# Streaming the second half of an adaLN weight beside a projection, letting DMA issues go first on GpSimd, and putting a layer norm's affine part last

## The chip, the cores and the metric

The kernel runs on all eight cores of one Trainium2 chip, with no traffic between the cores. Times are device microseconds of the slowest core. Before the change the time was 824.52 us, the median of three runs (823.72 to 826.96). An execution has now and then a slower state, in which the cores of one die or of both run at a lower granted clock; such runs are called slow here, are listed, and are not used for comparisons.

Engines: TensorE (PE in the profile, PEld its weight loads), VectorE (DVE), ScalarE (ACT), GpSimd (POOL) and SyncE (SP).

## The reference, cut to what matters

One layer of a flow-matching backbone. Per core: one latent sequence of 1024 tokens and two context sequences of 256, model width 1024, feed-forward width 2816.

```python
# mod = SiLU(cond) @ w_ada + b_ada             w_ada is 1024 x 6144: twelve slabs of 512 columns
sh1, sc1, g1, sh2, sc2, g2 = jnp.split(mod, 6, axis=-1)
h = x * (1 + sc1) + sh1                        # slabs 0 to 3
proj = h @ p['w_in']                           # q, k, v, g of four retention heads | z, x, B, C, dt of the SSD group
...                                            # retention heads; Mamba-2 SSD heads, a chunked scan over 64-token chunks
mix = jnp.concatenate([o_ret, o_ssd], axis=-1) @ p['w_out']
x = layer_norm(ALPHA * x + g1 * mix, p['ln1_g'], p['ln1_b'])       # g1: slabs 4, 5
h2 = x * (1 + sc2) + sh2                                           # slabs 6 to 9
ffn = (jax.nn.silu(h2 @ p['w_gate']) * (h2 @ p['w_up'])) @ p['w_down']
x = layer_norm(ALPHA * x + g2 * ffn, p['ln2_g'], p['ln2_b'])       # g2: slabs 10, 11
```

Outputs are the new context and latent activations and the final retention and SSD states of the context (oret and ossd in the profile).

## The kernel before

The program is written as a list of operations in one order, and a small list scheduler inside the kernel file orders them. It keeps one clock per engine, and each time it lets the engine take the ready operation with the lowest key (level, position in the list). From that it fixes, at build time, the order of each engine and all semaphore waits. Buffers are then placed in one SBUF arena by their planned lifetimes, and each reuse of bytes adds a dependency. A planned order that the chip doesn't follow in time is not mended at run time: an engine waits for the next instruction in its order (start_restored_wo_early below has a case of 7.18 us).

```python
def add(self, alts, reads, writes, table=None, after=()):
    o = Op(len(self.ops), alts, (self.level, len(self.ops)), self.tag)    # the key
...
def dma(self, eng, out, in_, after=(), is_out=False):
    v = out if isinstance(out, View) else in_
    o = self.add({eng: (0.9 if eng == POOL else 0.45, lambda e: e.dma_start(...))}, [in_], [out], after=after)
...
P.tag, P.level = "start", 0                     # constants, x, the first weights, their arithmetic
...
LV_EV, LV_MIX, LV_DENSE, LV_BG = 0, 1, 2, 3     # evictions, scans, dense products, background
```

The large weights come in as slabs, most of 128 x 4096 elements, cast from fp32 in memory to bf16 by DMAs that GpSimd issues, at level 3 after the start and at level 0 in it. GpSimd also does arithmetic: the SSD state updates at level 1, LN1's multiply and add at level 3. The parts that the change touches:

```python
ada_load(4, [last_mm[0]]);  ada_load(5, [last_mm[1]])      # after the last product of a w_in slab
gate_row(0, 0);  gate_row(0, 1)                            # gate1: 8 matmuls of 2 x 512 each
...
rrg, rstS = Ring("rg", 3, 512), Ring("stS", 1, 512)        # retention gate; staging of the final states
...
for h in range(4):                                          # context heads
    last_h.append(head(GA, h, head_load(GA, h, [...]), LV_DENSE))
    if h < 2:
        ada_load(6 + h, [last_h[h - 1] if h else last_mm[1]])
        ada_load(8 + h, [last_h[h - 1] if h else last_mm[2]])
        mod2(h)                                             # shift2 and scale2: 2 x 32 matmuls of 128 x 2
    else:
        ada_load(8 + h, [last_h[h - 1]])
        gate_row(1, h - 2)
wo_load(0);  wo_load(1)                                     # w_out, released by last_h[2]
...                                                         # SSD of the latents, latent heads, out projection
P.level = LV_BG
ln1 = P.buf("ln1", 2048)
P.dma(SP, ln1, brow(R_LN1G, 2048), after=[oB])
for g in (GA, GB):
    for t in TT[g]:
        tt(x1[t], x1[t], ln1[:, 0:1024], ALU.mult, POOL)    # LN1's affine part: 24 instructions of 128 x 1024
        tt(x1[t], x1[t], ln1[:, 1024:2048], ALU.add, POOL)
ffn("all", LV_DENSE, [[hb[4]], [hb[4]], [oB]])              # 11 gate/up slabs (w_gu)
```

## Time and profile before

| what | value | where from |
|---|---|---|
| time, median of 3 | 824.52 us | runs |
| cores | 811.3 to 822.5 us | the profile's list of cores |
| mean granted TensorE clock | 0.945 to 0.960 | the same |
| PE idle on the slowest core | 110.2 us | 822.5 - 712.3 |
| PE idle in the start, until the projections run | 39.1 us | median of the cores, PE timelines and windows |
| PE idle from there to the third w_gu issue / from there to PE's end | 43.2 / 17.0 us | the same |

The head of the page has PE's busy time and the span cut into forty slices of 20.6 us. A digit is the busy tenths of the slice; PEclk is the granted clock, DMA the mean share of the sixteen DMA engines.

```profile
PE 712.3 (87%) x4432; PEld 373.0 (45%) x4432; DVE 398.1 (48%) x810; ACT 295.2 (36%) x470; POOL 304.1 (37%) x353
...
PE   0199999997982679899999799499999999999994
...
PEclk9999899999895789899999899799999999999998
DMA  8997132003979695202813300632266450301111
```

PE has two holes after the start, at the thirteenth slice (247 to 267 us) and at the twenty-sixth (514 to 535 us), and in both the clock drops as well. The DMA engines are at three tenths or less in slices five to ten (82 to 206 us), and at six to nine tenths in the five after those. The chain of waits says the same by engine:

```profile
PE 77%; DMA 11%; DVE 5%; issue 4%; ACT 1%; POOL 1%; SPq 0%; DVEq 0%; POOLq 0%; ACTq 0%
```

### The profile page before, as it was taken

The numbers are of one execution on the slowest core, as the hardware profiler recorded it, in microseconds if no ns is written. First come the engines' busy times: TensorE is split into PE (matmuls) and PEld (weight loads), VectorE is DVE, ScalarE is ACT, GpSimd is POOL, SyncE is SP. The second block draws the span as 40 slices with busy tenths as digits, with TensorE's granted clock in tenths as the row PEclk, the third lists the DMA queues.
The fourth block names the chain that finished last, engine by engine and source line by source line (L and its number), as shares of the span: only waits on it lengthen the run. The fifth ranks groups of instructions, "written<-read, shape, count | busy, mean of one in ns | idle before, by whom it ended". The sixth has DMA issues, their size and how long they took to land.

```text
span 822.5 us, 13372 instructions; the slowest of 8 cores (811.3 to 822.5 us)
## 1 busy us (share of the span) xinstructions
PE 712.3 (87%) x4432; PEld 373.0 (45%) x4432; DVE 398.1 (48%) x810; ACT 295.2 (36%) x470; POOL 304.1 (37%) x353
## 2 busy tenths in 40 slices
PE   0199999997982679899999799499999999999994
PEld 0168555554560334565544444144444444444441
DVE  4326547489771228888857822012222222266644
ACT  3545665676451343364554611012111111022211
POOL 9300124398451102455412699100000000058665
PEclk9999899999895789899999899799999999999998
DMA  8997132003979695202813300632266450301111
GB/s 163 204 258 129 48 53 65 1 16 53 161 130 168 156 161 149 41 13 53 179 37 125 96 1 1 96 57 52 52 122 124 101 122 1 71 26 77 78 52 77
DMA packets 19907, 73.35 MB, mean 89 GB/s; under 512 B 6000, under 2 KB 8432, under 8 KB 14208
## 3 DMA queue, kind: packets, MB, share of 16 engines
q0 software_dynamic: 6192, 44.65, 31.9%
q1 hardware_dynamic: 13648, 27.85, 10.5%
q8 instruction: 37, 0.61, 0.3%
q14 instruction: 30, 0.25, 0.1%
HBM read 108.74 MB, written 8.40 MB: 142 GB/s over the span
## 4 chain that ended last, share of the span: by engine, by line
PE 77%; DMA 11%; DVE 5%; issue 4%; ACT 1%; POOL 1%; SPq 0%; DVEq 0%; POOLq 0%; ACTq 0%
PE psum L607 74%; DMA arena<-x 4%; DMA oret<-arena 4%; PE psum L610 3%; DVE arena L655 2%; ACT arena L632 1%; DMA arena<-w_ada 1%; DMA arena<-w_gu 1%; DVE arena L669 1%; POOL arena L655 1%; DVE arena L689 1%; DVE arena L661 0%; SPq L182 0%; DVE arena L680 0%; DVEq L501 0%
## 5 line engine op out<-in xcount | busy, mean ns | idle before, releaser
L607 PE MATMUL psum<-arena 128*128 128x512 bf16 (+7 forms) x4228 | 685.6, 321 | 85.4 <-DMA arena<-w_ada 20.4
L607 PEld LDWEIGHTS psum<-arena 128*128 128x128 bf16 (+1 forms) x4228 | 346.7, 101 | 420.2 <-issue 129.5
L655 POOL TENSOR_TENSOR arena<-arena 128x512 f32<-128x512 f32 (+5 forms) x203 | 248.6, 1244 | 189.7 <-DVE arena L661 71.7
L632 ACT ACTIVATE arena<-psum 128x512 bf16<-128x512 f32 (+1 forms) x198 | 111.3, 572 | 298.1 <-PE psum L607 286.8
L655 DVE TENSOR_TENSOR arena<-psum,arena 128x512 f32<-128x512 f32 (+4 forms) x208 | 128.2, 636 | 106.7 <-PE psum L607 87.0
L655 DVE TENSOR_TENSOR arena<-arena,psum 128x512 bf16<-128x512 bf16 (+2 forms) x124 | 82.9, 676 | 197.2 <-PE psum L607 181.6
L632 ACT ACTIVATE arena<-arena 128x512 f32<-128x512 f32 (+7 forms) x121 | 86.5, 732 | 166.0 <-DVE arena L669 131.9
L669 DVE SCALAR_TENSOR_TENSOR arena<-arena 128x1 f32<-128x1 f32 (+2 forms) x108 | 62.8, 588 | 18.8 <-POOL arena L655 12.8
L632 ACT ACT_TABLE_LOAD x40 | 51.3, 1283 | 30.8 <-PE psum L607 24.5
L632 ACT ACTIVATE arena<-psum,arena 128x512 bf16<-128x512 f32 (+3 forms) x75 | 47.2, 649 | 27.3 <-PE psum L610 19.0
L182 POOL DMA_DIRECT2D arena<-w_gu x11 | 6.1, 556 | 122.4 <-PE psum L607 116.8
L610 PE MATMUL psum<-arena 128*128 128x128 f32 (+1 forms) x204 | 30.8, 305 | 13.8 <-DMA arena<-x 8.2
L680 DVE CAST arena<-psum 128x512 bf16<-128x512 f32 (+2 forms) x38 | 21.8, 590 | 31.0 <-PE psum L607 23.8
L655 DVE TENSOR_TENSOR arena<-arena 128x1 f32<-128x1 f32 (+9 forms) x74 | 31.7, 432 | 8.9 <-ACT arena L632 2.8
L610 PEld LDWEIGHTS psum<-arena 128*128 128x128 f32 (+1 forms) x204 | 26.8, 157 | 17.8 <-issue 15.9
L661 POOL TENSOR_SCALAR arena<-arena 128x128 bf16<-128x128 f32 (+2 forms) x42 | 23.2, 563 | 17.1 <-ACT arena L632 10.7
L182 POOL DMA_DIRECT2D arena<-w_ada x12 | 7.2, 605 | 54.7 <-PE psum L607 53.7
L182 POOL DMA_DIRECT2D arena<-w_down x4 | 2.1, 529 | 61.3 <-PE psum L607 61.2
L182 POOL DMA_DIRECT2D arena<-w_in x11 | 6.3, 574 | 49.6 <-PE psum L610 24.7
L661 DVE TENSOR_SCALAR arena<-arena 128x128 bf16<-128x128 f32 (+5 forms) x73 | 19.4, 304 | 9.5 <-ACT arena L632 6.8
L689 DVE TENSOR_SCALAR arena<-psum,arena 128x512 bf16<-128x512 f32 x21 | 16.6, 806 | 14.3 <-PE psum L610 14.2
L1174 DVE COPY_PREDICATED psum<-arena,psum 128x512 f32<-128x512 uint16 x24 | 16.6, 691 | 8.9 <-PE psum L607 8.8
(18 smaller groups left out, 60.7 us busy)
## 6 DMA issues: line engine op xcount, KB each, us to landing
arena<-w_ada POOLq DMA_DIRECT2D x12, 1024.0 KB, 17.8
arena<-x SPq DMA_DIRECT2D x24, 512.0 KB, 18.1
arena<-w_in POOLq DMA_DIRECT2D x11, 1024.0 KB, 22.4
arena<-w_gu POOLq DMA_DIRECT2D x11, 1024.0 KB, 12.5
arena<-w_down POOLq DMA_DIRECT2D x4, 1408.0 KB, 15.8
y<-arena SPq DMA_DIRECT2D x11, 512.0 KB, 2.6
arena<-gsc SPq DMA_DIRECT2D x4, 512.0 KB, 9.4
arena<-w_out POOLq DMA_DIRECT2D x2, 1024.0 KB, 19.5
```

Of the source, the lines that this page charges most:

```text
L182: o = self.add({eng: (0.9 if eng == POOL else 0.45, lambda e: e.dma_start(out=R(out), in_=R(in_)))}, [in_], [out], after=after)
L607: return P.add({PE: (c, lambda e: e.matmul(R(out), lhsT=R(lhsT), rhs=R(rhs), start=start, stop=stop))}, [lhsT, rhs], [out])
L610: return P.add({PE: (0.12, lambda e: e.transpose(out=R(out), in_=R(in_), identity=R(ident_f)))}, [in_, ident_f], [out])
L632: fn = lambda e: e.activation(out=R(out), in_=R(in_), func=func, **{k: R(v) for k, v in kw.items()})
L655: fn = lambda e: e.tensor_tensor(out=R(out), in0=R(in0), in1=R(in1), op=op)
L661: fn = lambda e: e.tensor_scalar(out=R(out), in0=R(in0), scalar1=R(s1), scalar2=None, op0=op0)
L669: fn = lambda e: e.scalar_tensor_tensor(out=R(out), in0=R(in0), scalar=R(scalar), in1=R(in1), op0=op0, op1=op1, **{k: R(v) for k, v in kw. ...
L680: alts[g] = (vcost(g, out, [in_], "copy"), lambda e: e.tensor_copy(out=R(out), in_=R(in_)))
L689: lambda e: e.tensor_scalar(out=R(out), in0=R(in_), scalar1=R(scale), scalar2=R(bias), op0=ALU.mult, op1=ALU.add))
L1174: P.add({DVE: (0.7, lambda e, eb=eb, ef=ef, mk_=mk_: e.copy_predicated(R(eb), R(mk_), R(ef)))}, [mk_, ef, eb], [eb])
```

## The change

The intent is to read the second half of w_ada (slabs 4 to 11) while the z projection and the SSD stage keep PE busy and the DMA engines idle, rather than in a heap beside the context heads; to keep loads from standing behind arithmetic on GpSimd; and to move LN1's affine part out of the way of the gate/up loads. Two rings and the release of w_out are adjusted.

```diff
     def dma(self, eng, out, in_, after=(), is_out=False):
         v = out if isinstance(out, View) else in_
+        lv, self.level = self.level, 0.5
         o = self.add({eng: ...}, [in_], [out], after=after)
+        self.level = lv
...
-    ada_load(4, [last_mm[0]])
-    ada_load(5, [last_mm[1]])
-    gate_row(0, 0)
-    gate_row(0, 1)
+    used = [last_mm[0], last_mm[0]]
+
+    def ada_next(s):
+        ada_load(s, [used[-2]])
+
+    for half in range(2):
+        ada_next(4 + half)
+        used.append(gate_row(0, half))          # gate_row and mod2 now return their last products
+    for half in range(2):
+        ada_next(6 + half)
+        ada_next(8 + half)
+        used += mod2(half)
+    for half in range(2):
+        ada_next(10 + half)
+        used.append(gate_row(1, half))
...
-    rsq, rrg, rqf = Ring("sq", 2, 512, BF16), Ring("rg", 3, 512), Ring("qf", 3, 512, BF16)
+    rsq, rrg, rqf = Ring("sq", 2, 512, BF16), Ring("rg", 2, 512), Ring("qf", 3, 512, BF16)
...
-    rstS, rS1, rS0 = Ring("stS", 1, 512), ...
+    rstS, rS1, rS0 = Ring("stS", 4, 512), ...
...
-        wo[half] = slab_load("wo%d" % half, w_out_d[half], 4096, after=[last_h[2]])...
+        wo[half] = slab_load("wo%d" % half, w_out_d[half], 4096, after=[last_h[3]])...
...                                             # in the loop of the context heads:
-        if h < 2:
-            ada_load(6 + h, ...); ada_load(8 + h, ...); mod2(h)
-        else:
-            ada_load(8 + h, ...); gate_row(1, h - 2)
...
     P.dma(SP, ln1, brow(R_LN1G, 2048), after=[oB])
+    P.level = 4
     for g in (GA, GB):
```

More of the change, by code (lines that the diff above doesn't have):

```diff
@@ L973, in gate_row @@
         for kt in range(8):
-            mm(ps[0:2, :], scv3[:, kt, :], wv[:, kt, :], kt == 0, kt == 7)
+            o = mm(ps[0:2, :], scv3[:, kt, :], wv[:, kt, :], kt == 0, kt == 7)
         P.level = LV_EV
@@ L979, in gate_row @@
         gdma[(which, half)] = P.dma(SP, gsc_d[which * 2:which * 2 + 2, hs], gs[0:2, 0:512])
+        return o
     def mod2(half):
         P.level = 1.2
+        n0 = len(P.ops)
         sh2[half] = mod_cols("sh2_%d" % half, 6 + half, "dense")
@@ L994, in mod2 @@
         scale2[half], bias2[half] = s_, b_
+        return [P.ops[n0 + 31], P.ops[n0 + 64]]
     def to_tm(g):
@@ L1220, in build @@
     rPT = Ring("PT", 2, 2048, BF16)
-    rsq, rrg, rqf = Ring("sq", 2, 512, BF16), Ring("rg", 3, 512), Ring("qf", 3, 512, BF16)
+    rsq, rrg, rqf = Ring("sq", 2, 512, BF16), Ring("rg", 2, 512), Ring("qf", 3, 512, BF16)
     epsb = P.buf("epsb", 1)
     memset(epsb, EPS)
-    rstS, rS1, rS0 = Ring("stS", 1, 512), Ring("S1", 2, 256, BF16), Ring("S0", 2, 256)
+    rstS, rS1, rS0 = Ring("stS", 4, 512), Ring("S1", 2, 256, BF16), Ring("S0", 2, 256)
     def ret_unit(h, ck, o0, nt, W, qT, kT, v3, gT, cross):
@@ L1335, in wo_load @@
         P.level = LV_BG
-        wo[half] = slab_load("wo%d" % half, w_out_d[half], 4096, after=[last_h[2]])[0].rearrange("p (k n) -> p k n", k=8)
+        wo[half] = slab_load("wo%d" % half, w_out_d[half], 4096, after=[last_h[3]])[0].rearrange("p (k n) -> p k n", k=8)
     ln2 = P.buf("ln2", 2048)
@@ L1462, in build @@
         last_h.append(head(GA, h, head_load(GA, h, [(last_mm[1], last_mm[2], last_h and last_h[0], last_h[1:] and last_h[1])[h]]), LV_DENSE))
-        if h < 2:
-            ada_load(6 + h, [last_h[h - 1] if h else last_mm[1]])
-            ada_load(8 + h, [last_h[h - 1] if h else last_mm[2]])
-            mod2(h)
-        else:
-            ada_load(8 + h, [last_h[h - 1]])
-            gate_row(1, h - 2)
     wo_load(0)
```

## The prediction

> **What bounds the kernel now.** The time is 824.52 us, the profiled span 822.5 us on core 3. I read first the page: TensorE (PE) is busy 87% and the chain that ended last runs on PE for 77%. So the question is where PE is not busy, or busy at a low clock. Waits by releaser, PE as the waiter, before any ordering in time:
>
> ```profile
> PE psum L607 <- DMA arena<-w_ada: 20.4, 4, 7.3
> ...
> PE psum L607 <- DMA arena<-w_gu: 10.8, 1, 10.8
> ...
> PE psum L607 <- POOL arena L655: 9.1, 4, 4.1
> PE psum L607 <- DMA oret<-arena: 9.0, 1, 9.0
> ...
> PE psum L607 <- DMA arena<-w_in: 4.8, 1, 4.8
> ```
>
> The columns are total us, times, longest. A total mixes places, so I went to the PE timeline (start, busy; in brackets the idle time before):
>
> ```profile
> 206.95 8.87 PE L607 MATMUL psum<-arena 128*2 128x512 bf16 x58 [2.86 <-DMA arena<-w_ada]
> ...
> 251.81 0.99 PE L607 MATMUL psum<-arena 128*128 128x2 bf16 x32 [3.48 <-DMA arena<-w_ada]
> 257.60 2.29 PE L607 MATMUL psum<-arena 128*128 128x512 bf16 x5 [4.79 <-DMA arena<-w_in]
> 268.84 9.74 PE L607 MATMUL psum<-arena 128*128 128x128 bf16 x67 [8.95 <-DMA oret<-arena]
> ...
> 529.68 30.55 PE L607 MATMUL psum<-arena 128*128 128x512 bf16 x132 [10.81 <-DMA arena<-w_gu]
> ```
>
> Two of the four w_ada waits lie at 23 and 31 us, in the start, which this change leaves alone (14.1 us); only 2.86 + 3.48 us are of the second half. The windows show the stages (span, then busy time of PE, weight loads, DVE, ACT, POOL; granted clock, DMA share, GB/s):
>
> ```profile
> 110.00:176.00 66.00, 65.61 (x497) 37.23 (x496) 39.18 (x64) 41.00 (x71) 32.83 (x37) 1.00 0.20 42
> 176.00:240.00 64.00, 55.83 (x553) 33.28 (x551) 56.43 (x92) 35.53 (x63) 45.63 (x57) 0.92 0.58 95
> 240.00:285.00 45.00, 21.14 (x203) 12.48 (x202) 10.53 (x26) 14.73 (x26) 7.75 (x13) 0.73 0.85 160
> 285.00:345.00 60.00, 50.88 (x300) 26.39 (x301) 35.23 (x78) 19.23 (x31) 13.13 (x15) 0.86 0.58 114
> ...
> 470.00:530.00 60.00, 49.19 (x229) 22.19 (x228) 12.07 (x18) 9.70 (x16) 47.90 (x24) 0.94 0.14 23
> 530.00:812.00 282.00, 281.46 (x1296) 127.09 (x1294) 91.45 (x184) 50.07 (x81) 68.69 (x63) 0.99 0.33 72
> ```
>
> From 110 to 176 us PE is full while the DMA engines are 80% idle; from 240 to 285 us it is the reverse. The slabs are read late and all at once. POOL's timeline says why:
>
> ```profile
> 195.03 1.56 POOL L655 TENSOR_TENSOR arena<-arena 128x512 f32<-128x512 f32 x2
> 196.55 0.66 POOL L182 DMA_DIRECT2D arena<-w_ada  x1
> 197.20 0.55 POOL L182 DMA_DIRECT2D arena<-w_in  x1
> ...
> 460.00 56.22 POOL L655 TENSOR_TENSOR arena<-arena 128x1 f32<-128x1 f32 x25 [1.78 <-DVE arena L661]
> 519.47 1.68 POOL L182 DMA_DIRECT2D arena<-w_gu  x3 [3.26 <-PE psum L607]
> ```
>
> The issues at 196.55 have no idle time before them: they stood behind arithmetic in POOL's fixed order, and so did three w_gu loads, behind 56 us of LN1's multiply and add. PE ran out of gate/up weights at 518.9 us, before the first of those was even issued.
>
> **What the Trainium skill says.** "TensorE: Matmul & The Clock Gate", section Part 1 (The HAM clock gate), has PE at half clock after an idle window of about 3.4 us and full again after one of busy time. This trace agrees: the granted clock is 0.51 and 0.50 in the slices 250 to 260 and 260 to 270 us, and after the w_gu wait 132 matmuls took 30.55 us, 0.231 each, against 281.79 us / 1296 = 0.217 in the chain after it. So a removed wait gives back more than itself. The same section would have a sustained all-core load run at 13/16 clock; here 530 to 812 us is granted 0.99, so I fear no penalty for a denser PE. "GPSIMD Engine Reference", section 2.1, describes one instruction stream dispatched in order, which is the line above: a load cannot pass an add. "DMA: Bandwidth & Descriptors", section Issuing engines are not separate DMA queues, says that all issuers share 16 engines and interleave: the oret write issued on SP at 237.79 us, behind three slabs issued in the 5 us before it, held PE until 268.84.
>
> **The change part by part.** No arithmetic is added or removed; eight w_ada slabs, 24 LN1 instructions and all loads change places.
>
> 1. *FFN start.* The w_gu loads no longer stand behind LN1. The fourth slab can go when the first is used up. A slab is 96 matmuls x 0.217 = 20.8 us of PE, so that is about two slabs, some 40 us, before it is needed; landing took 10.07 us alone. The wait of 10.81 goes, and so does the slow clock after it, 132 x (0.231 - 0.217) = 1.8. LN1's 56 us move into the following 210 us before the down projection (norms from about 725 us), where POOL does almost nothing. Gain 12 to 13 us, near certain; the other cores show the same wait, 8.9 to 14.0 us.
>
> 2. *Slabs 5 to 11 of w_ada and the head weights.* At the start, four slabs follow one another at about 8 us each (PE waits end at 15.19, 23.44, 31.29). Slab 4 goes at 111.8 us already; the rest now follow in pairs, each released by the product two before it. Four pairs at 16 us plus a PE slot, some 72 us, end near 185 us; with two head slabs, near 200. The 110 to 176 window has 53 us of idle DMA, 176 to 200 another 20: it just fits. In the old order the last w_ada went at 279 us. Their products (32 small matmuls in 0.99 us; four gate rows of 8 x 0.217 = 1.7 us) only change places. Head 0's weights go before 196.55 us, and later heads have the queue to themselves.
>
> 3. *The stage 176 to 345 us.* Idle PE time is 8.2 + 23.9 + 9.1 = 41.2 us. Low clock, by 10 us slices (busy x (1 - clock)) from 200 to 310 us: 2.3 + 1.3 + 1.6 + 0.6 + 1.9 + 1.0 + 1.9 = about 10.5. Together about 52 us that are not work. Directly removed: 2.86 + 3.48 + 4.79 (loads) and 8.95 (oret: its staging buffer goes from one to four, so the matmul that needs it does not wait for the write), 20 us, with perhaps 7 of the clock. Of the remaining 21 us idle, waits like 3.94 and 4.08 us on POOL at a retention unit's end are there because no other matmul stood ready in PE's order; with the next head's weights in, some get filled. I take 5 to 10. Sum 32 to 37 us; less 4 for costs below: about 31.
>
> 4. *Small costs.* The rg ring goes from three to two (units come some 10 us apart and its chain is about 4 us: nothing, perhaps 1 us). w_out waits for the last context head rather than the third: two slabs landed in 19.5 us (median), against some 20 us of SSD and latent-head work: 0 to 4 us. About ten issues of 0.6 us move into POOL's dense stretch (170 to 190 us: 10.00 and 9.97 busy of 10): up to 4 us of state updates delayed.
>
> Sum: 12.5 + 31 = 43.5; 824.5 - 43.5 = 781.
>
> **Rivals.**
> *SSD slows down.* PE order and POOL order are both fixed. If a slab lands later than planned, PE stalls in a stretch that was full, and a load on POOL that waits for that product holds up the state updates behind it. Also, SSD's state loads and writes (3.0 and 3.1 us now) would sit behind slabs as oret did. For it: POOL is full at 170 to 190 us, oret took 31 us. Against: SSD has head matmuls beside it. It would eat 15 to 25 of part 3: 796 to 806.
> *DVE becomes the bound.* It is busy 56.4 of 64 us at 176 to 240. But over 176 to 345 it has 102 us of 169; shortened by 33 it is 75% of the time. Locally it caps what SSD can hide: then only the 20 direct us come, 793.
> *The transfers were hidden anyway*, and PE waits next on what stood behind. For the start's w_ada waits this is so by position; for 240 to 285 us, with DVE and ACT both under a third busy, it is not. If it were, only part 1 remains: 812.
> *All gaps close*: 52 + 12.5 gives 760.
>
> **Range and chances.** Part 1 is worth 12.5 +- 2; part 3 runs from 12 (SSD slowed) to 46. So 764 to 801, centre 780. The 2% line is 808; to miss it part 3 must give less than 4 us: 5%. Slower by over 2% would need a new stall of 30 us: 1%.
>
> **What would show it.** Right: no PE wait on w_gu, and POOL's LN1 instructions spread after 470 us; DMA share at 110 to 176 us up from 0.20 to about 0.9 and no w_ada issue after about 200 us; no PE wait on oret; PE idle between 176 and the end of that stage under 20 us, clock there above 0.95; the FFN matmuls starting about 30 us earlier, at near 440. Wrong: new PE waits on w_ada or sssd at 120 to 200 us, POOL idle on PE before its issues with DVE waiting on POOL, or a PE wait on w_out after the context heads.

## The result, and the profile after

The changed kernel took 773.07 us, the median of four runs (769.09 to 774.86). The kernel before took 825.74 beside it (median of four, 823.72 to 827.31). The ratio is 0.9357, with a 95% interval of 0.9309 to 0.9405: faster, and within the predicted range. Ratios here are the mean time of one kernel's fast runs over that of the other's in the same rounds, so not quite the ratio of the medians that are quoted. One ratio does not follow from this, that of ln_waits_for_transposes; it is spoken of there. All outputs are right.

The head of the page of the changed kernel, on its slowest core (core 2), and the line of its chain of waits:

```profile
PE 688.2 (89%) x4358; PEld 367.7 (48%) x4432; DVE 394.3 (51%) x806; ACT 290.7 (38%) x466; POOL 310.3 (40%) x361
...
PE   0059999899999988899997999999999999999993
...
PEclk9979889999999999999999999999999999999998
DMA  9985805698337575226326032333775504012112
...
PE 81%; DMA 7%; DVE 5%; issue 4%; POOL 1%; ACT 1%; SPq 0%; DVEq 0%; POOLq 0%; ACTq 0%
```

Both holes are gone and the clock stays at 9 from the seventh slice to the last but one. The DMA engines work at slices seven to ten (116 to 193 us), where they had been nearly idle. But the third slice, 39 to 58 us, now has a 5: a hole at the start that wasn't there. PE's busy time fell from 712.3 to 688.2 with the same work (4432 weight loads in both). Part of that is the better clock, and part that 74 matmul records are missing here, so this difference isn't used below.

PE's waits by releaser, on the same core (total us, times, longest):

```profile
PE psum L609 <- DMA arena<-w_ada: 22.6, 2, 12.8
PE psum L612 <- DMA arena<-x: 15.5, 1, 15.5
PE psum L609 <- DVE arena L657: 8.7, 5, 5.5
...
PE psum L609 <- DMA ossd<-arena: 2.2, 1, 2.2
...
PE psum L609 <- DMA arena<-w_in: 1.4, 1, 1.4
```

There is no wait on w_gu, none on oret, and the two on w_ada are both in the start (12.79 and 9.81 us in the PE timeline). After the start only 2.2 us on an SSD write and 1.4 us on a head slab are waits on a transfer on this core. No core waits on oret or w_gu; one waits 0.3 us on w_ada, and cores 1, 5 and 6 wait 1.8 to 2.2 us on w_out, which the prediction had named as a sign of being wrong. The windows of the middle, with the columns of the prediction's windows:

```profile
110.00:176.00 66.00, 62.74 (x499) 34.92 (x508) 34.97 (x74) 37.44 (x62) 22.63 (x26) 0.94 0.68 116
176.00:240.00 64.00, 60.41 (x539) 36.04 (x544) 48.59 (x77) 39.24 (x69) 45.48 (x55) 1.00 0.51 92
240.00:285.00 45.00, 40.21 (x380) 25.80 (x385) 38.87 (x68) 29.39 (x50) 22.88 (x28) 1.00 0.65 138
285.00:345.00 60.00, 55.62 (x390) 31.66 (x395) 54.18 (x106) 27.70 (x45) 32.54 (x37) 1.00 0.42 88
```

The DMA share of the first row went from 0.20 to 0.68. The same moments hold other work now, since everything comes earlier, so the rows are read as a whole: PE's idle time in the other three is 3.6 + 4.8 + 4.4 = 12.8 us where it had been 41.2, and the granted clock of each is 1.00 where it had been 0.92, 0.73 and 0.86. The first row lost a little: its idle time went from 0.4 to 3.3 us and its clock from 1.00 to 0.94. GpSimd's timeline shows where the loads went:

```profile
121.67 1.26 POOL L183 DMA_DIRECT2D arena<-w_ada  x2 [22.94 <-PE psum L609]
...
183.01 0.59 POOL L183 DMA_DIRECT2D arena<-w_ada  x1
...
425.83 16.20 POOL L657 TENSOR_TENSOR arena<-arena 128x1024 f32<-128x1024 f32 x7 [1.31 <-DMA arena<-rows]
441.98 0.62 POOL L183 DMA_DIRECT2D arena<-w_gu  x1
442.62 13.86 POOL L657 TENSOR_TENSOR arena<-arena 128x1024 f32<-128x1024 f32 x6
458.24 0.59 POOL L183 DMA_DIRECT2D arena<-w_gu  x1 [1.76 <-PE psum L609]
```

The last w_ada load is issued at 183.0 us, where it had been at 279. The w_gu loads go between LN1's instructions rather than after all of them.

The cores differ by several us, so I compare the stages by the median of the eight cores. The next table is worked out from each core's timelines: the moment at which the projections start, the fifth w_ada load is issued, and so on, in us.

| kernel | projections start | 5th w_ada | last w_ada | w_out | first latent head's slab | 1st w_gu | 3rd w_gu | PE's end |
|---|---|---|---|---|---|---|---|---|
| before | 48.7 | 110.1 | 275.9 | 276.5 | 278.0 | 386.8 | 447.4 | 807.8 |
| changed | 57.1 | 118.9 | 178.2 | 267.2 | 249.6 | 347.0 | 408.6 | 755.1 |
| changed, again | 56.3 | 117.2 | 175.8 | 265.5 | 247.3 | 344.5 | 406.7 | 755.6 |

The start lost 8.8 us up to the fifth w_ada load. From there to the third w_gu load it was 337.3 us and is 289.7: 47.6 less. From there to PE's end it was 360.4 and is 346.5: 13.9 less. The sum is 8.8 - 47.6 - 13.9 = -52.7, which is the end's 807.8 to 755.1.

So the time came out some 7 us below the prediction, and two errors of opposite sign lie behind that: the middle gained more than foretold, and the start, which I had called untouched, lost. That they nearly cancelled is luck. PE's timeline there, of the kernel before (core 3) and of the changed one (core 2):

```profile
31.29 0.99 PE L607 MATMUL psum<-arena 128*128 128x2 bf16 x32 [6.86 <-DMA arena<-w_ada]
40.46 3.65 PE L610 MATMUL psum<-arena 128*128 128x128 f32 x16 [8.18 <-DMA arena<-x]
```

```profile
23.59 0.99 PE L609 MATMUL psum<-arena 128*128 128x2 bf16 x32 [9.81 <-DMA arena<-w_ada]
40.09 3.32 PE L612 MATMUL psum<-arena 128*128 128x128 f32 x16 [15.51 <-DMA arena<-x]
43.24 0.94 PE L609 MATMUL psum<-arena 128*128 128x2 bf16 x32
49.64 0.99 PE L609 MATMUL psum<-arena 128*128 128x2 bf16 x32 [5.46 <-DVE arena L657]
51.05 3.65 PE L612 MATMUL psum<-arena 128*128 128x128 f32 x16 [0.42 <-DVE arena L657]
```

The groups of 32 are the products of the first four w_ada slabs, the groups of 16 the transposes of x. Before, the third of the four products ran at 31.29 us, ahead of the transposes; now it stands behind them in PE's order, and the fourth then waits 5.46 us on DVE. Nothing in the start was edited. But the start's operations have level 0, and the line `self.level = 0.5` put its DMAs behind level 0 rather than ahead, and the scheduler drew another order of everything from there.

### The profile page after: what moved, and what is told of

It is laid out like the page before. It is cut to its first block, busy times and chain, and to the rows that moved or that the text cites. A ratio compares the mean times of both kernels' runs of the same rounds, so it can differ in the third digit from the quotient of the medians.

```text
span 770.4 us, 13287 instructions; the slowest of 8 cores (764.3 to 770.4 us)
## 1 busy us (share of the span) xinstructions
PE 688.2 (89%) x4358; PEld 367.7 (48%) x4432; DVE 394.3 (51%) x806; ACT 290.7 (38%) x466; POOL 310.3 (40%) x361
## 4 chain that ended last, share of the span: by engine, by line
PE 81%; DMA 7%; DVE 5%; issue 4%; POOL 1%; ACT 1%; SPq 0%; DVEq 0%; POOLq 0%; ACTq 0%
PE psum L609 78%; DMA arena<-x 5%; PE psum L612 2%; DVE arena L657 2%; DMA arena<-w_in 2%; POOL arena L657 1%; ACT arena L634 1%; DVE arena L671 1%; DMA ossd<-arena 1%; DVE arena L691 1%; SPq L183 0%; DVE psum L1190 0%; DVE arena L682 0%; POOL arena L663 0%; DVEq L503 0%
## 5 line engine op out<-in xcount | busy, mean ns | idle before, releaser
L609 PE MATMUL psum<-arena 128*128 128x512 bf16 (+9 forms) x4154 | 662.6, 316 | 51.0 <-DMA arena<-w_ada 22.6
L609 PEld LDWEIGHTS psum<-arena 128*128 128x128 bf16 (+3 forms) x4228 | 342.4, 100 | 367.7 <-issue 72.4
L657 POOL TENSOR_TENSOR arena<-arena 128x512 f32<-128x512 f32 (+5 forms) x207 | 252.1, 1236 | 181.0 <-ACT arena L634 59.8
L634 ACT ACTIVATE arena<-psum 128x512 bf16<-128x512 f32 (+2 forms) x197 | 110.0, 569 | 257.4 <-PE psum L609 236.7
L657 DVE TENSOR_TENSOR arena<-psum,arena 128x512 f32<-128x512 f32 (+5 forms) x208 | 127.4, 635 | 63.2 <-PE psum L609 52.0
L634 ACT ACTIVATE arena<-psum,arena 128x512 bf16<-128x512 f32 (+3 forms) x72 | 45.0, 645 | 34.2 <-PE psum L612 23.4
L612 PE MATMUL psum<-arena 128*128 128x128 f32 (+1 forms) x204 | 28.7, 295 | 18.9 <-DMA arena<-x 15.5
L682 DVE CAST arena<-psum 128x512 bf16<-128x512 f32 (+2 forms) x39 | 23.6, 620 | 30.0 <-PE psum L609 23.4
L657 DVE TENSOR_TENSOR arena<-arena 128x1 f32<-128x1 f32 (+9 forms) x70 | 27.8, 403 | 8.5 <-ACT arena L634 4.1
L691 DVE TENSOR_SCALAR arena<-psum,arena 128x512 bf16<-128x512 f32 x24 | 18.8, 808 | 22.9 <-PE psum L612 22.6
L663 DVE TENSOR_SCALAR arena<-arena 128x1 f32<-128x1 f32 (+7 forms) x69 | 16.5, 281 | 8.3 <-ACT arena L634 5.4
```

Source lines behind the costliest of these rows:

```text
L609: return P.add({PE: (c, lambda e: e.matmul(R(out), lhsT=R(lhsT), rhs=R(rhs), start=start, stop=stop))}, [lhsT, rhs], [out])
L612: return P.add({PE: (0.12, lambda e: e.transpose(out=R(out), in_=R(in_), identity=R(ident_f)))}, [in_, ident_f], [out])
L634: fn = lambda e: e.activation(out=R(out), in_=R(in_), func=func, **{k: R(v) for k, v in kw.items()})
L657: fn = lambda e: e.tensor_tensor(out=R(out), in0=R(in0), in1=R(in1), op=op)
L663: fn = lambda e: e.tensor_scalar(out=R(out), in0=R(in0), scalar1=R(s1), scalar2=None, op0=op0)
L682: alts[g] = (vcost(g, out, [in_], "copy"), lambda e: e.tensor_copy(out=R(out), in_=R(in_)))
```

## The experiments

My first theory: the middle's gain is the priority of the DMA issues and the stream together, the end's is LN1 off the w_gu loads, and the lost start is a plain cost that can be had back. The rivals: the rings do a large part of it (the oret wait was the longest of the middle); and the lost start is absorbed later. The runs were made each on one chip beside runs of the kernel before. Fast runs only, unless said. The kernel before had four slow runs, of 843.38, 881.71, 911.02 and 942.05 us.

| run | median or fast runs, us | ratio to before, 95% interval |
|---|---|---|
| after_same | 773.32 (770.86 to 773.58) | 0.9358, 0.9333 to 0.9383 |
| start_restored | 775.36 (774.01 to 776.75) | 0.9390, 0.9363 to 0.9416 |
| only_ln_late | 813.59 (807.50 to 814.79) | 0.9838, 0.9794 to 0.9881 |
| only_rings | 822.41, 825.89, 815.00; slow 864.76 | 0.9943, 0.9878 to 1.0009 |
| all_but_stream | 790.21, 785.38, 784.99; slow 909.88 | 0.9545, 0.9503 to 0.9586 |
| all_but_priority | 798.38, 799.76, 802.37; slow 816.72 | 0.9706, 0.9674 to 0.9738 |
| all_but_rings | 771.89 (770.86 to 777.64) | 0.9377, 0.9334 to 0.9420 |
| start_restored_wo_early | 790.92, 789.68, 789.00; slow 895.63, 888.13 | 0.9575, 0.9548 to 0.9601 |
| ln_waits_for_transposes | 768.42, 776.23, 774.17; slow 782.01, 790.43, 816.82 | 0.9437, 0.9392 to 0.9482 |
| start_restored_ln_waits | 773.00 (769.35 to 778.18) | 0.9392, 0.9354 to 0.9430 |
| wo_early_ln_waits | 773.25, 774.29, 772.57; slow 867.94, 786.93 | 0.9387, 0.9359 to 0.9416 |
| changed_wo_early_ln_waits | 783.75 (783.15 to 784.52) | 0.9514, 0.9489 to 0.9538 |

And where in the program the time of each lies, from the medians of the eight cores of the profiled run, in us (a stage is the difference of two medians):

| run | projections start | 5th to last w_ada | 5th w_ada to 3rd w_gu | 3rd w_gu to PE's end |
|---|---|---|---|---|
| before | 48.7 | 165.8 | 337.3 | 360.4 |
| after_same | 56.3 | 58.6 | 289.5 | 348.9 |
| start_restored | 49.5 | 57.8 | 297.0 | 346.9 |
| only_ln_late | 49.5 | 166.8 | 338.5 | 348.6 |
| only_rings | 49.0 | 159.3 | 326.8 | 355.4 |
| all_but_stream | 56.3 | 138.7 | 303.2 | 346.4 |
| all_but_priority | 49.5 | 101.6 | 325.7 | 346.9 |
| all_but_rings | 56.1 | 58.5 | 288.5 | 347.2 |
| start_restored_wo_early | 49.7 | 57.9 | 300.2 | 357.7 |
| ln_waits_for_transposes | 55.9 | 58.0 | 287.0 | 345.8 |
| start_restored_ln_waits | 48.6 | 59.0 | 297.3 | 344.4 |
| wo_early_ln_waits | 49.4 | 58.4 | 301.1 | 345.2 |
| changed_wo_early_ln_waits | 56.3 | 58.3 | 303.1 | 345.4 |

**after_same.** The changed kernel unaltered, to know its spread.

> The changed kernel unaltered, as the yardstick for the other runs of this call. Expected as recorded before: ratio to the kernel before 0.931 to 0.941, near 773 us; the projection's first 128x512 matmul at 56 to 58 us (50.3 us in the kernel before).

773.32 us, every run within 3 us. Its core spans, 764.5 to 769.8, are like those of the first profile (764.3 to 770.4): the gain of the middle and of the end and the loss at the start are a property of the kernel, not of one execution.

**start_restored.** A DMA issued at level 0 stays at 0, so the start has its old order.

```diff
-        lv, self.level = self.level, 0.5
+        lv, self.level = self.level, min(self.level, 0.5)
```

> Changed kernel, but a DMA keeps its level where that is below 0.5 (the start's level 0), so that PE's order at the start is again three w_ada products, then the x transposes, then the fourth. Theory: in the changed kernel the level 0.5 alone turned the start's order, put ACT's and DVE's mask work between the products and the projections, and costs 6 to 8 us there; expected projection start 48 to 51 us, time 764 to 768 us, ratio to before 0.925 to 0.930. Rival: x lands at 40 us in both, and what follows (the GA prep and conv chain, the first w_ada issue) takes the gain back; then the projection starts earlier but the time stays 771 to 775 us.

775.36 us, no faster than the changed kernel. The edit did what it should: in the PE timeline of core 7 the projections start at 50.5 us, and by the table they start 6.8 us earlier (49.5 against 56.3).

```profile
50.46 15.97 PE L609 MATMUL psum<-arena 128*128 128x512 bf16 x98 [1.39 <-DVE arena L691]
...
275.84 9.12 PE L609 MATMUL psum<-arena 128*128 128x512 bf16 x49 [2.62 <-DMA arena<-w_out]
```

The lead is still 7.9 us at the first latent head's slab (239.4 against 247.3), and 0.6 us at the first w_gu load. So it is lost in the latent heads. The second line shows a wait of 2.6 us on w_out; such a wait isn't new, since three cores of the changed kernel have one of 1.8 to 2.2 us. PE's idle time is 9.0 against 4.7 us between the fifth w_ada and w_out, 6.3 against 4.8 up to the first w_gu, and 1.9 against none up to the third: 17.2 against 9.5 us together, about as much as the lead. By releaser (means of the cores) most of what was added is waits for DVE, 11.6 against 6.7 us; waits on head slabs and w_out are 3.1 against 1.2. The theory that the start's loss is a plain cost fell. That the lead is lost later, mostly in waits for DVE, is shown; what in the redrawn order makes DVE late is not.

**only_ln_late.** The kernel before with LN1's instructions at level 4, nothing else.

```diff
     P.dma(SP, ln1, brow(R_LN1G, 2048), after=[oB])
+    P.level = 4
     for g in (GA, GB):
```

> Kernel before with LN1's multiply and add at level 4 and nothing else. Theory: only the w_gu loads behind LN1 cost the FFN's start; no PE wait on w_gu, 12 to 13 us less, 811 to 814 us, everything before 450 us unchanged. Rival: the fourth slab is held by something else (the third slab's late issue at 449.9 us, or memory reuse), then a wait of 5 us or more stays and the time is 818 to 825 us; or LN1 in the way of the down projection: time as before.

813.59 us against 826.44: 12.8 us. The ratio's interval, 0.9794 to 0.9881, leaves out 1 but not the 2% line, so the record's verdict is "unclear" as to 2%; that it is faster is clear. The PE timeline of core 5 has, at the place of the 10.8 us wait on w_gu, one unbroken piece:

```profile
471.83 88.44 PE L607 MATMUL psum<-arena 128*128 128x512 bf16 x409
```

By the table nearly all of it is in the last stage (360.4 to 348.6). This is the end's part of the prediction, alone.

The prediction's reading of the old wait needs one correction. On core 3 LN1 ended at 516.2 us, and GpSimd then idled 3.26 us before it issued w_gu (the last line of the prediction's GpSimd timeline); on six of the eight cores it idled 0.9 to 4.1 us there, on cores 1 and 7 not at all. In the program as built, the first of these three issues is the fifth slab's. It was given the bytes of the third slab and so waits for that slab's last product, and the fourth slab, which PE needs, is issued after it. So what was last on six cores was this order. With LN1 out of the way it is not drawn: the built program then issues the slabs in sequence.

There is more on `P.level = 4`. In the changed kernel the line that does it here does nothing: with all DMAs at level 0.5 they pass LN1's instructions at level 3 as well. I built the changed kernel without `P.level = 4` and compared the orders of the two programs: they are the same on all five engines, so it was not run.

**only_rings.** The kernel before with the two rings of the change (stS 1 to 4, rg 3 to 2), nothing else.

> Kernel before with the state staging ring 1 to 4 and the rg ring 3 to 2, nothing else. Theory: the wait of 8.95 us of PE on the oret write goes, and most of it is gained, 815 to 819 us. Rival: PE then waits for the slabs that are landing in the same 20 us (w_in, w_ada), the transfers set the pace, and the time stays 822 to 826 us.

The time is the same (0.9943, and the interval holds 1). The cores disagree, which the time hides: spans run from 796.6 to 821.4 us, where the kernel before has 811.3 to 822.5. The median core ends 16.8 us earlier (791.0 against 807.8), but the slowest sets the time. On six cores PE waits 3.6 to 4.9 us on oret, where the eight cores of the kernel before wait 7.7 to 10.9; on core 5, 16.8; on core 2, 23.4, nearly all of it in one place:

```profile
299.15 14.17 PE L607 MATMUL psum<-arena 128*128 128x512 bf16 x86 [21.77 <-DMA oret<-arena]
```

With four staging buffers the wait on the previous write is gone, but in the program as built a later buffer takes the bytes of each of the first three, and its first writer waits for that write to leave. The write behind the 21.77 us was issued at 247.05 us with two slabs of w_ada and two of w_in in flight, and took 52.0 us to land. So the wait is moved, and on two cores it grew.

**all_but_stream.** The changed kernel with w_ada's second half back at its old places in the list; the priority, the rings and w_out's release stay.

> Changed kernel with the w_ada loads and products of the second half back where they were (beside the context heads); priority of the DMA issues, LN1 late, rings and w_out's later release stay. Theory: the stream is worth most of the middle; the FFN gain (12.5 us) and some from head loads going first stay: 790 to 802 us, DMA share at 110 to 176 us below 0.5, and PE waits on w_ada or w_in again after 200 us. Rival: POOL's backlog was the whole cause, and first place for the issues suffices: 771 to 780 us.

The fast runs are 784.99 to 790.21, ratio 0.9545 against 0.9358: the stream is worth 0.0187 x 825 = 15 us. The window of core 1 from 110 to 176 us is idle for the DMAs again:

```profile
110.00:176.00 66.00, 66.00 (x453) 36.44 (x452) 35.02 (x68) 45.15 (x72) 24.54 (x28) 0.98 0.26 50
```

The middle takes 303.2 us against 289.5, which is nearly all of the 15.

**all_but_priority.** The changed kernel with DMAs at the level of the code around them, as before.

```diff
-        lv, self.level = self.level, 0.5
         o = self.add({eng: ...}, [in_], [out], after=after)
-        self.level = lv
```

> Changed kernel without the level 0.5 for DMAs (they are ordered by LV_BG as before); stream, LN1 late, rings stay. Theory: the loads stand behind the SSD state updates on POOL again, the last w_ada goes after 190 us instead of 178 and the head weights late, PE waits on w_in or w_ada at 200 to 270 us: 782 to 800 us; its start is the old one (projections at 48 to 50 us), which does not help in the end. Rival: with the stream early in the program its issues find POOL free anyway: 768 to 777 us.

The fast runs are 798.38 to 802.37, ratio 0.9706: the priority is worth 0.0348 x 825 = 29 us, net of the start, which this run has back (49.5 us). In the middle alone it is 325.7 against 289.5. PE of core 7, and GpSimd's last w_ada load on the same core:

```profile
168.40 16.58 PE L607 MATMUL psum<-arena 128*128 128x256 bf16 x132 [10.32 <-DMA ossd<-arena]
```

```profile
213.44 0.64 POOL L182 DMA_DIRECT2D arena<-w_ada  x1
214.52 0.54 POOL L182 DMA_DIRECT2D arena<-w_in  x1 [0.44 <-issue]
```

The stream alone makes the loads possible early, but on GpSimd they still stand behind arithmetic: the last w_ada goes at 211 us (median) rather than 176, and the head slabs behind it. And an SSD write behind slabs holds PE for 10.32 us (9.1 to 10.3 on every core; it was issued at 153.2 us, just after two slabs), which is the first rival of the prediction, come true in this variant.

Two more that would belong here could not be tried: the priority alone, and the priority with the stream but without the rings and the later w_out, do not fit the arena (213,408 and 217,920 bytes per partition are needed of 212,800).

**all_but_rings.** The changed kernel with the rings as before (stS 1, rg 3). The instruction order of all engines is that of the changed kernel.

> Changed kernel with one staging buffer and three rg buffers as before; the order of instructions is the same on all engines, only the waits differ. Theory: the oret writes land in a few us once no slab reads are piled up beside them, so the ring is worth little here: 771 to 776 us, PE wait on oret under 2 us. Rival: the write still takes 10 us or more beside the later head slabs and PE waits 8 us: 779 to 785 us.

771.89 us and 0.9377 against 0.9358: the intervals overlap, so the rings are worth nothing that these runs can tell. The rival that gives them a large part fell, and with it a step of my prediction. No core waits on oret here. The first two writes are issued with one slab in flight, not three, and land after 5 to 6 and 10 to 13 us, where the first took 29 to 31 us in the kernel before; so one staging buffer is enough. The run is a weak test of four separate buffers, though: in the changed kernel as built, three of the four were given the same bytes.

**start_restored_wo_early.** As start_restored, and w_out released by the third context head as before, against the 2.6 us wait on w_out.

```diff
-        wo[half] = slab_load("wo%d" % half, w_out_d[half], 4096, after=[last_h[3]])...
+        wo[half] = slab_load("wo%d" % half, w_out_d[half], 4096, after=[last_h[2]])...
```

> The restored start with w_out released by the third context head again instead of the fourth. Theory: restored start lost its 7 us between the w_out issue and the latent heads (PE wait on w_out, 79 us became 84), so an earlier w_out gives some back: 763 to 770 us on the slowest core. Rival: that stretch is limited by DVE and by the instruction order as drawn by the scheduler, not by w_out: 771 to 778 us.

789.00 to 790.92 us: 15 us slower than start_restored, worse than either theory allowed. The last stage takes 357.7 us rather than 346.9. Core 0, at the last latent tile's norm and transposes, on GpSimd, DVE and PE:

```profile
428.76 17.73 POOL L657 TENSOR_TENSOR arena<-arena 128x1024 f32<-128x1024 f32 x9 [7.25 <-DMA arena<-rows]
...
434.02 0.16 DVE L671 SCALAR_TENSOR_TENSOR arena<-arena 128x1 f32<-128x1 f32 x1 [7.18 <-POOL arena L657]
...
436.68 7.60 DVE L691 TENSOR_SCALAR arena<-arena 128x512 f32<-128x512 f32 x3
...
444.43 0.87 PE L612 MATMUL psum<-arena 128*128 128x128 f32 x3 [11.96 <-DVE arena L691]
```

Three DVE instructions that take 0.5 us each elsewhere took 7.60 us together, while GpSimd ran LN1's products, and PE waited 11.96 us for them. Before that DVE had waited 7.18 us for a small norm step that stands behind two of LN1's products in GpSimd's order, so the hold is not all of PE's wait here. I looked for the same in the changed kernel. It is there, smaller, on five of the eight cores (and on six in the kernel before): on core 7 of after_same, GpSimd has LN1 from 415.9 us, and DVE's next two groups are

```profile
416.15 2.15 DVE L671 SCALAR_TENSOR_TENSOR arena<-arena 128x1 f32<-128x1 f32 x1 [0.93 <-POOL arena L657]
...
418.41 4.95 DVE L691 TENSOR_SCALAR arena<-arena 128x512 f32<-128x512 f32 x2
```

2.15 us for an instruction of one column, and 2.5 us for one of 512; PE waited 3.3 us for them. That gave the new theory: LN1's instructions on GpSimd hold DVE, about one GpSimd instruction each time, at the one place where PE waits for DVE; its rival was that the slow DVE is a matter of that variant's placement.

**ln_waits_for_transposes.** The changed kernel, with the load of LN1's rows (and so all of LN1's affine part) released by the last transposes of the feed-forward input, rather than by the out projection. By the comparison of the built programs only GpSimd's order differs from the changed kernel's.

```diff
-    P.dma(SP, ln1, brow(R_LN1G, 2048), after=[oB])
+    P.dma(SP, ln1, brow(R_LN1G, 2048), after=[last_tr[1]])      # last_tr: the transposes into h2T, noted as they are made
```

> Changed kernel, the row of LN1's gain loaded only after the last transpose before the FFN, so that POOL's 24 LN1 instructions start some 8 us later; order on PE, DVE, ACT and SP is the same. Theory: while POOL runs LN1's 1024-wide products, DVE's instructions that read and write SBUF alone are held up (2.47 us instead of 0.55, and 2.15 instead of 0.16) in five of eight cores, ahead of the last transposes; without it those cores lose the 7 us of slow DVE and gain 4 to 6 us: 768 to 771 us on the slowest core, no DVE instruction over 1.3 us there. Rival: PE waits there for the norm's chain anyway (a row of short DVE, POOL and ACT steps), time 771 to 775 us.

DVE's line on core 7, at the same place:

```profile
416.45 0.16 DVE L671 SCALAR_TENSOR_TENSOR arena<-arena 128x1 f32<-128x1 f32 x1 [0.93 <-POOL arena L657]
416.72 1.00 DVE L691 TENSOR_SCALAR arena<-arena 128x512 f32<-128x512 f32 x2
```

0.16 rather than 2.15 us, 0.50 each rather than 2.47. On no core does a DVE instruction of that stage take over 1.3 us. So the hold is shown, and its cause is GpSimd's work at that moment, since nothing else was moved. The last stage is 345.8 us against 348.9, but the fast runs (768.42, 776.23, 774.17) lie around those of the changed kernel: three us of the median core don't show in the slowest one. Three of the six runs were slow. The ratio, 0.9437, is higher than these three fast runs give (their mean is 772.94 us, against some 824: 0.938), so I don't use it, and that this variant is a little slower can't be ruled out.

**start_restored_ln_waits.** Both: `min(self.level, 0.5)` and LN1 after the transposes.

> Both repairs: the start as in the kernel before, and LN1 held back until the last transpose. Theory: each repair acts at its own place; start_restored was 775 us and has 4.6 us of slow DVE there: 770 to 772 us, and the start's 7 us stay lost to the other instruction order. Rival: the two add to what the start promised, 762 to 767 us.

773.00 us, six fast runs, ratio 0.9392. In the median core the end comes at 751.3 us against 755.6, but the cores spread from 753.9 to 772.9 us. Core 5, the slowest, in the SSD stage:

```profile
129.11 14.44 PE L609 MATMUL psum<-arena 128*128 128x256 bf16 x102 [1.25 <-DMA ossd<-arena]
...
167.24 14.80 PE L609 MATMUL psum<-arena 128*128 128x256 bf16 x120 [5.21 <-DMA ossd<-arena]
```

Core 0, which ends 19 us earlier, has at the same place one piece of 64 us without a wait. The two waits on the write of an SSD state are 6.5 of those 19 us. Elsewhere such waits are 1.8 us at most, and core 1, which has none, is ten us slower than core 0; where the rest lies I didn't trace.

**wo_early_ln_waits.** start_restored_wo_early with LN1 after the transposes: the direct test of why that run was slow.

> The run that fell to 791 us (start restored, w_out released early) with LN1 held back. Theory: 9.8 to 12 us of slow DVE and a PE wait of 12 us were LN1's doing; that wait falls below 3 us and the time to 777 to 782 us, still slower than the changed kernel because of what lies before. Rival: DVE was late there for another reason: 786 to 792 us.

772.57 to 774.29 us, against 789.00 to 790.92: some 16 us back by moving LN1 alone. The last stage goes from 357.7 to 345.2 us. So LN1's work at that moment is the cause of that run's loss. How much of it is the hold on DVE and how much the norm step behind LN1 in GpSimd's own order, this run can't tell, since it moves both. And w_out's early release by itself costs this start nothing that the time shows (773.25 against 773.00 for start_restored_ln_waits).

**changed_wo_early_ln_waits.** The changed kernel (its own start), w_out early, LN1 after the transposes.

> The changed kernel (its own start) with w_out released by the third context head as before, LN1 held back; to be set against ln_waits_for_transposes, which differs in w_out's release alone. Theory: w_out's later release is no cost (w_out lands during latent and SSD work) and the early one fills the queue when the context heads need it: 772 to 785 us, slower than the pair run by 3 us or more. Rival: early is better, as PE waits up to 2 us on w_out in the changed kernel: 765 to 768 us.

783.75 us, against 768 to 776 for the fast runs of the same without the early w_out: some 10 us worse (6 by the ratios). By the table the loss is in the middle (303.1 against 287.0). So what an early w_out costs depends on the start's order: nothing beside the restored one, ten us beside the changed one. It is no fixed cost of the transfer, then; that it comes from the order that the scheduler draws is likely and not shown.

No variant beats the changed kernel by more than the runs' spread. The nearest, start_restored_ln_waits and wo_early_ln_waits, are at 773.0 and 773.3 us (median of the fast runs) against 773.3; all_but_rings is at 771.89, but its ratio is no lower than the changed kernel's.

## Why the prediction was right or wrong

**The end (its part 1): right.** 12 to 13 us foretold; 12.8 us alone in only_ln_late, and 13.9 and 11.5 us in the last stage of the two profiles of the changed kernel. The cause that it names holds, with the correction under only_ln_late: the w_gu loads no longer stand behind LN1, nor in the order that LN1's place had drawn. The means is another: in the changed kernel the DMA level does it, and `P.level = 4` is idle.

**The stream (part 2): right in kind, one figure too high.** The last w_ada was to be issued by about 200 us, and it is issued at 178. The DMA share of 110 to 176 us was to be about 0.9 and is 0.68. No w_ada wait above 0.7 us came in the SSD stage.

**The middle (part 3): right in direction, too small.** 31 us net was foretold; 47.6 us came. The terms, before against after_same, medians of the cores: PE's idle time from the fifth w_ada to the first w_gu went from 42.4 to 9.5 us, that is 33 us. The prediction had 20 us of direct waits and "5 to 10" for the rest, so that the rest was 13. The low clock was undersized too, "perhaps 7 of the clock": counted from the trace's clock intervals, PE lost 8.0 and 6.2 us while busy in these two stages (medians of the cores), and none and 0.5 after, so the term is 14. On core 3 it is 14.8 us, where the prediction's slices have 10.5, mostly because they end at 310 us and leave out a stretch at half clock from 335.6 to 342.4 us. So 33 + 14 = 47 us, against 47.8 in after_same, and the "less 4 for costs" didn't show. So the rival "All gaps close" was nearly right for the middle, and the one of DVE as a bound fell: DVE is busy 54.18 of 60 us in the last window of the middle while PE is idle for 4.4. The rival that the transfers were hidden anyway (812 us) fell with the time.

What carries it isn't what part 3 names first. The priority is worth 29 us and the stream 15, each by taking it out of the whole. Counted up from only_ln_late (0.9838), with the rings and the later w_out let in, the priority gives 24 us (0.9545) and the stream 11 (0.9706), so each is worth more beside the other. The head slabs gain with them, as the pages' lists of DMA issues show, first of the kernel before, then of the changed one (size, then median us from issue to landing):

```profile
arena<-w_in POOLq DMA_DIRECT2D x11, 1024.0 KB, 22.4
```

```profile
arena<-w_in POOLq DMA_DIRECT2D x11, 1024.0 KB, 9.7
```

**The oret step: failed.** "8.95 (oret: its staging buffer goes from one to four, so the matmul that needs it does not wait for the write)". The wait did go, but not by the ring: all_but_rings has one buffer and the same time, and only_rings has four, and PE waits up to 21.77 us on a write of oret. Where the ring alone did help, on six cores of only_rings, some 5 us of the wait went. What removed it was fewer slabs beside the write, one rather than three.

**The small costs (part 4).** The rg ring costs nothing (all_but_rings). The later w_out shows as a wait of 1.8 to 2.2 us on three cores, within the 0 to 4 us foretold, and was the right choice: early, it is some 10 us worse with this start.

**The step that failed: "in the start, which this change leaves alone".** The projections start 8.4 us later (57.1 against 48.7), on every core. I read the diff's `self.level = 0.5` as raising the loads of level 3, and did not ask what it does to operations at a lower level than that: the start's DMAs had level 0 and were lowered. start_restored shows that this line does it, since `min` brings the projections back to 49.5 us. It also shows that the end doesn't come earlier for it. So the prediction left out a loss of 8.8 us in the sum of the stages, and the undersized middle hid that, by luck; to take the loss away again bought nothing.

**The first rival, SSD writes behind slabs,** is real and small here: 2.2 us on core 2 and none to 1.6 on the others. Without the priority it is 9.1 to 10.3 us in one wait on every core.

Left open: why PE waits longer for DVE after the restored start, what of start_restored_wo_early's loss is the hold on DVE alone, and whether a larger ring of state buffers would free the slow cores of the SSD writes.

## What to carry to other kernels

Where loads are issued from an engine that also computes, look in its timeline for issues with no idle time before them: they stand behind arithmetic, and letting them pass was the largest single gain here (29 us). A wait on a small write can be a symptom of what stands before it in the DMA engines, so count what is in flight with it before giving it more buffers, and look in the built program whether the buffers of a ring have bytes of their own. When a priority is set to a fixed value, ask for every class of operation whether it goes up or down, and with a scheduler that draws the whole order anew, don't expect a stage's gain to arrive at the end: measure it on all cores, since the slowest sets the time.

## What the Trainium skill lacked or had wrong

- "SBUF — State Buffer", section SBUF: two separate sides, says that the port pair shared by GpSimd and DVE is an exclusive lock, held for a whole instruction. The runs agree, and give it a size: beside GpSimd's 128 x 1024 products (16.20 us for seven, 2.3 each) a DVE tensor_scalar of 128 x 512 took 2.47 us rather than 0.50, and a one-column scalar_tensor_tensor 2.15 rather than 0.16; it cost PE 3.3 us in one wait on core 7 of after_same. The page has no time for what a short DVE instruction pays.
- "DMA: Bandwidth & Descriptors", section Issuing engines are not separate DMA queues, has transfers of several issuers interleave. It lacks what a small write then pays: the oret write took 31 us behind three slabs (prediction), and another held PE for 21.77 us in only_rings, while with one slab in flight the first write landed in 5 to 6 us and one staging buffer was enough.
- "TensorE: Matmul & The Clock Gate", section Part 1 (The HAM clock gate), lowers the clock after idle windows. In the kernel before, core 3, the mean clock is 0.68 from 80 to 90 us (half from 79.6 to 86.4) although PE is reported busy for all of it; 16 fp32 matmuls of 128 x 16 come just before, and then 128 x 512 products at 0.43 us each rather than 0.21. What lowered the clock there no run shows. The page's limit of 13/16 of the clock for dense load on several cores did not hold in the fast runs: core 7 of after_same is busy for all of 530 to 720 us at a granted clock of 1.00. In the slowest runs (942.05 us of the kernel before, 909.88 of all_but_stream) the four cores of one die have a mean clock of 0.80 to 0.82, which is near 13/16; whether it is that limit isn't shown.
